# A streaming-encoder block with SwiGLU: where silu's product and the feature sums of the pair behind stand among the quarter products

## Chip, core and metric

One core of a Trainium2 chip runs the whole block in one launch. The metric is the device time of one execution in microseconds. The kernel before took 1066.19 us (median of 3 runs, 1064.51 to 1068.32).

## Reference

The block is one layer on 1024 tokens of width 1024, all in float32. The change lies in the second half, the SwiGLU:

```python
h2 = rmsnorm(x, norm2_g[layer])
gate = jnp.einsum('bsd,df->bsf', h2, w_gate[layer])
up = jnp.einsum('bsd,df->bsf', h2, w_up[layer])
x = x + jnp.einsum('bsf,fd->bsd', jax.nn.silu(gate) * up, w_down[layer])
```

`d` is 1024 and `f` is 2816. Ahead of it stand the norm, the input projection, the attention with forget gates, the pooling mixer and the output projection, and behind it a last norm.

## The kernel before

Every float32 operand of a matmul is split into a high part (a copy by ScalarE, L120) and a low part (the difference, by VectorE, L121); a product is three matmuls (L161 to L163: high by high, high by low, low by high). Such a pair of parts of one weight operand is called a page. There are three page buffers, so a page takes the place of the one three pages earlier, once TensorE has read that.

Gate and up are made with Strassen's method in Winograd's form: seven products of blocks, called P1 to P7, with sums of blocks as operands. The 2816 features go in eleven pairs of 128-wide groups, `j` from 0 to 10. For a pair the raw weights of gate and up arrive by DMA (`gu_raw`, issued by SyncE), GpSimd makes the four weight sums s1 to s4 of the pair ahead (`gu_sums`, L1091; s4 is the last), and the pages of the products follow one by one (`next_page`, two steps ahead in the list `todo`). Index n is 0 for gate and 1 for up.

The products accumulate in PSUM banks: c1 takes P1, P6 and P5, c3 takes P7 and P4. Between them ScalarE copies what is needed to SBUF (`snap`, L1154: sP1, sU2 and sU4 for n = 0 and 1). From banks and copies `corner` makes the features: VectorE adds bank and copy (L1178 for gate, L1180 for up), ScalarE applies silu (L1179) and GpSimd multiplies (`done`, L1181). This gives h22 and h21. h11 is multiplied at L1314. h12 is multiplied by VectorE (L1340) after silu (L1338), in `features`. GpSimd then makes the four feature sums f1 to f4 for the down projection (`feature_sum`, L1190: f1 needs h12 and h22, f2 needs f1 and h11, f3 needs h11 and h12, f4 needs h21 and f2). `spill` stores features in DRAM through ScalarE's DMA queue. Copies, features and sums share a ring of 11 buffers; the copies of sU2 have one buffer for each n, and silu of h21 is written over the copy of sU2 with n = 0.

The products P2 and P3 are done once more by the same method, as seven quarter products Q1 to Q7 with 256 columns (`fine_product`). Their results go through three banks called fineA (Q1, Q6, Q5, Q3 in turn), fineB (Q7, then Q4) and fineC (Q2). A bank keeps accumulating, so VectorE adds each stand of it to the copies in SBUF (L1288), and the next quarter product on that bank must wait for this addition. The operand quarters are summed in place by VectorE (`fine_sums`, L1245: one sum in part "a", ahead of the page P2a; three in part "b", ahead of the page P2b).

From pair 3 on (`BOTH = 3`) a pair runs the order LAST, with P2's quarters woven into P6, and P3's into P4:

```python
LAST = ("P1", "P7", "P2a", "P6", "P2b", "P5", "P3a", "P4", "P3b")
```

At step P2a TensorE does Q1, Q2, Q7, a quarter of P6, Q4, another quarter of P6 and Q6; at step P6 the second half of P6 and Q5.

Each engine runs its instructions in the order of its queue. A planner sets that order ahead of time; `tc.issue_after(ins)` demands that an instruction stands behind `ins` in the queue of the same engine. Before the change, the work around step P1 of a pair was issued so: `features(j - 1)` first, then page P2a with its sum "a"; page P6 at step P7; the three sums "b" at step P2a. GpSimd multiplies h22 (pairs 3 to 9) and h21 (pairs 2 to 10) behind s4.

Of the kernel before, what the change touches and what calls it, by code (L numbers as in the profile page):

```python
# [30 lines left out]
NG = NF // 2  # L31
# [14 lines left out]
def tile_kernel(  # L46
# [16 lines left out]
    nc = tc.nc  # L63
# [24 lines left out]
    def bank(name, tag, bufs, n=1):  # L88
# [11 lines left out]
        out=wmask[:, S - P :],  # L100
# [16 lines left out]
    mark = {}  # L117
# [683 lines left out]
    op = op_g.__enter__()  # L801
# [273 lines left out]
    BOTH = 3  # L1075
# [81 lines left out]
    feats = {}  # L1157
    ready = {}
    pending = []
# [7 lines left out]
    def corner(j, name, key, src, to):  # L1167

        h = feature(j, name, to)
        if key == "sU2" and j >= BOTH - 1:  # L1170
            q = snaps[j, key, 0]
        else:
            q = wk_tile("q" if key else "e2", 1, f"q{name}_{j}")
        if key is None:
            nc.scalar.activation(out=q, in_=banks[src, 0], func=AF.Silu)
            nc.vector.tensor_tensor(out=h, in0=banks[src, 1], in1=q, op=ALU.mult)
        else:
            nc.vector.tensor_tensor(out=q, in0=banks[src, 0], in1=snaps[j, key, 0], op=ALU.add)  # L1178
            nc.scalar.activation(out=q, in_=q, func=AF.Silu)  # L1179
            mark[name, j] = nc.vector.tensor_tensor(out=h, in0=banks[src, 1], in1=snaps[j, key, 1], op=ALU.add)  # L1180
            done = lambda: nc.gpsimd.tensor_tensor(out=h, in0=h, in1=q, op=ALU.mult)  # L1181
            if name == "h22" and BOTH <= j < NG - 1:
                pending.append(done)
            else:
                with tc.issue_after(mark["s4"].ins) if name == "h21" and j >= BOTH - 1 else ExitStack():
                    done()

    def feature_sum(j, name, key, a, b, op):
        t = feature(j, name, key)
        nc.gpsimd.tensor_tensor(out=t, in0=feats[a], in1=feats[b], op=op)  # L1190

    QTR = (slice(0, 256), slice(256, 512))
    fine = {}
# [137 lines left out]
    def features(j, *behind):  # L1331

        if j:
            acc = [snaps[j, "sU4", n] for n in range(2)]
            with ExitStack() as order:
                for ins in behind:
                    order.enter_context(tc.issue_after(ins.ins))
                nc.scalar.activation(out=acc[0], in_=acc[0], func=AF.Silu)  # L1338
            with tc.issue_after(mark["page"].ins):
                nc.vector.tensor_tensor(out=acc[1], in0=acc[1], in1=acc[0], op=ALU.mult)  # L1340
            feats["h12"] = acc[1]
        feature_sum(j, "f1", "P5", "h12", "h22", ALU.add)
        feature_sum(j, "f2", "P6", "f1", "h11", ALU.subtract)
        feature_sum(j, "f3", "P7", "h11", "h12", ALU.subtract)
        if j:
            feature_sum(j, "f4", "P3", "h21", "f2", ALU.subtract)

# [69 lines left out]
    def next_page(j, k):  # L1417
        if (j, k) not in pages:
            if k[-1] in "ab":
                pages[j, k] = fine_page(j, k[:2], k[-1])  # L1420
            else:
                pages[j, k] = gu_page(f"gu{j}_{k}", operands[j][k])
        if j + 1 < NG:
            if k in ("P3", "P3a"):
                gu_raw(j + 1, 0)
            if k == "P4":
                gu_raw(j + 1, 1)
            if k == ("P3b" if j else "P4"):
                operands[j + 1] = gu_sums(j + 1)
                while pending:  # L1430
                    with tc.issue_after(mark["s4"].ins):
                        pending.pop(0)()

    PACE = {(1, "P1"): 3, (1, "P2"): 3, (2, "P1"): 2, (2, "P2"): 2, (2, "P6"): 3, (2, "P7"): 3}
    waiting = []
    for i, (j, k) in enumerate(todo):
        shown = mark["page"]
        if j >= BOTH and k == "P2a":
            fine_sums(j, "P2", "b")
        elif i + 2 < len(todo) and (j < BOTH or k != "P1"):  # L1440
            with ExitStack() as order:
                if j >= BOTH and k == "P3b":
                    order.enter_context(tc.issue_after(mark["add"].ins))
                if j >= BOTH and k in ("P7", "P6", "P2b", "P5"):
                    if k == "P5":
                        fine_sums(j, "P3", "b")
                    for name in ("page", "hi") + (("sum",) if k in ("P2b", "P5") else ()):
                        order.enter_context(tc.issue_after(mark[name].ins))
                next_page(*todo[i + 2])
            if j >= BOTH and k == "P6":  # L1450
                with tc.issue_after(mark["page"].ins):
                    fine_sums(j, "P3", "a")
            if k == "P2b":
                mark["P3a"] = mark["page"], mark["hi"]
        waiting.append(spills[:])
        spills.clear()
        if j < BOTH:
            while len(waiting) > 1:
                with tc.issue_after(mark["hi"].ins), tc.issue_after(mark["snap"].ins) if j == 2 else ExitStack():
                    spill(waiting.pop(0))  # L1460
        elif k in ("P7", "P3a", "P4", "P3b"):
            rest = sum(waiting, [])
            due = [e for e in rest if e[1] < j and (k != "P7" or e[0] in ("P1", "P4"))][: 8 if k == "P3b" else 2]
            waiting[:] = [[e for e in rest if e not in due]]
            with tc.issue_after(mark["hi"].ins):
                spill(due)
        if i == 1:
            product(j, k, 0, (0, 1))
            with tc.issue_after(mark["turn", ORDER[-1]].ins):
                product(j, k, 0, (2, 3))  # L1470
                product(j, k, 1)
        elif k in window[j]:
            step, little, whole = window[j][k]
            acc = [snaps.get((j, dict(P2="sP1", P3="sU4")[little], n)) for n in range(2)]
            deep = j >= BOTH and (j, little) != (NG - 1, "P3") or (j, k) == (BOTH - 1, "P3b")
            for piece in NEXT[k] if deep and k in NEXT else (PIECES2 if deep else PIECES)[step]:
                with tc.issue_after(mark["mm"].ins):
                    if isinstance(piece, str):
                        fine_product(j, little, piece, acc)
                    elif isinstance(piece[0], str):  # L1480
                        product(j + (k == "P3b"), *piece)
                    else:
                        product(j, whole, *piece)
                if (k, piece) == ("P2a", "Q7"):
                    with tc.issue_after(mark["Q7"].ins):
                        next_page(j, "P2b")
        elif i:
            for n in range(2):
                with tc.issue_after(mark["mm"].ins) if j >= BOTH or j == BOTH - 1 and k != "P1" else ExitStack():
                    product(j, k, n)  # L1490
        if (j, k) == (NG - 1, "P3b"):
            last_features = lambda j=j, k=k: after(j, k)
        else:
            if j >= BOTH and k == "P1":
                features(j - 1)
                with tc.issue_after(mark["add"].ins), tc.issue_after(mark["h21", j - 1].ins):
                    next_page(*todo[i + 2])
            after(j, k)
        if j == NG - 1:
            if k == "P1":  # L1500
                for par in range(2):
                    down_raw(0, par)
            if k == "P6":
                for par in range(2):
                    down_load(par)
            if k == "P2b":
                for key in ("P5", "P6", "P7", "P4"):
                    down_sum(0, key)
            if k == "P3a":
                with tc.issue_after(mark["add"].ins), tc.issue_after(mark["hi"].ins):  # L1510
                    down_page(0)
        if (j, k) == (0, "P4"):
            t = const.tile([P, 2, 2, 256], R, tag="wmask", bufs=1, name="fine1_b22")
            q7 = small(wk, "e2", "fine3h_b22"), small(xw, "junk2", "fine3l_b22")
            finer += fine_steps("b22", (t[:, 0, :, :], t[:, 1, :, :]), q7, ("e0", "e1"))
        if (j, k) == (BOTH - 2, "P3b"):
            q5, q7 = ([small(wk, f"g{n + m}", f"fine{n}{m}_b21") for m in range(2)] for n in (2, 4))
            finer += fine_steps("b21", q5, q7, ("g0", "g1"))
        for _ in range(min(PACE.get((j, k), 2 if j < 2 else 0), len(finer))):
            with tc.issue_after((shown if j == 2 else mark["page"] if j else mark["h22", 0]).ins):  # L1520
                finer.pop(0)()
        pages.pop((j, k))
# [184 lines left out]
```

## Time and profile before

| | |
|---|---|
| median of the runs | 1066.19 us |
| the profiled execution's own time | 1069.82 us |
| its span, first to last instruction | 1068.0 us |
| TensorE busy | 1035.7 us (97%) |
| VectorE busy | 804.0 us (75%) |
| ScalarE busy | 470.6 us (44%) |
| GpSimd busy | 408.5 us (38%) |
| mean granted TensorE clock | 0.986 |

The page of the profile gives busy times over the whole span. PE is TensorE, PEld its weight loads, DVE VectorE, ACT ScalarE, POOL GpSimd, SP SyncE; a q behind a name is the engine's DMA queue. In rows of waits stand the waiting instruction, what it waited for, the total in us, the number of times and the longest. Rows of stretches give the start and end, the length, busy time and instructions of PE, PEld, DVE, ACT and POOL, then the granted clock, the share of DMA and GB/s. Rows of the timeline give start, duration, engine, line, operation, output and inputs, and in brackets the idle time ahead with what ended it. In names the buffer numbers are left out: `gu_P` is a bank or a page of a product, `r` raw weights, `s` a weight sum, `sn_sU` and `sn_sP` copies, `f` and `h` features, and `fineB_6P` is the bank fineB in pair 6.

### The profile page before, as it was taken

The page shows a single profiled execution, that of the slowest core. Times are in us where ns is not written, and L with a number is a line of the kernel's source. Part 1 is how long each engine was busy: PE and PEld are TensorE (multiplying, and loading weights), DVE is VectorE, ACT ScalarE, POOL GpSimd, SP SyncE. Part 2 cuts the span into 40 slices and gives each one's busy share as a digit, 9 for nine tenths or more (in the row PEclk, how much of TensorE's full clock was granted, in tenths as well). Part 3 has the DMA queues.
Part 4 walks back from the last instruction along what each step waited for, and adds up shares of the span by engine and source line. Part 5 has one row for each costly group of instructions (what it writes and reads, how often), then busy time and mean ns, then how long its engine had stood idle before and what let it go on. Part 6 is the DMA issues. An engine that isn't in the chain of part 4 may idle for free.

```text
span 1068.0 us, 15171 instructions
## 1 busy us (share of the span) xinstructions
PE 1035.7 (97%) x5428; PEld 886.4 (83%) x5428; DVE 804.0 (75%) x1222; ACT 470.6 (44%) x759; POOL 408.5 (38%) x319
## 2 busy tenths in 40 slices
PE   9999999999999999999998998988989999999997
PEld 8988888998888888887787887877877888888886
DVE  7465566676885598979767767778678999888887
ACT  7334365665674276344233232432342433333445
POOL 4450121213452150844734826637538530000035
PEclk9999999999999999999999989998999999999999
DMA  6224334234931251423141332332216684354424
GB/s 243 51 64 140 84 95 103 60 100 103 331 92 50 91 168 55 141 72 108 41 129 60 109 119 69 109 111 69 97 60 226 225 317 147 119 178 147 149 89 158
DMA packets 108795, 130.28 MB, mean 122 GB/s; under 512 B 8040, under 2 KB 71024, under 8 KB 108720
## 3 DMA queue, kind: packets, MB, share of 16 engines
q1 hardware_dynamic: 97216, 108.18, 32.3%
q10 hardware_dynamic: 10784, 19.16, 4.7%
q0 software_dynamic: 720, 1.97, 0.5%
q8 instruction: 43, 0.70, 0.3%
q14 instruction: 32, 0.26, 0.1%
HBM read 86.29 MB, written 33.03 MB: 112 GB/s over the span
## 4 chain that ended last, share of the span: by engine, by line
PE 77%; DVE 8%; POOL 5%; issue 4%; DMA 3%; ACT 1%; SPq 0%; POOLq 0%; ACTq 0%; DVEq 0%
PE d L161 6%; PE d L163 6%; PE d L162 6%; PE gu_P L161 6%; PE gu_P L162 6%; PE gu_P L163 6%; POOL s L1091 4%; PE po L657 3%; PE tp L643 3%; PE qk L162 3%; PE qk L161 3%; PE qk L163 3%; PE o L162 3%; PE o L163 3%; PE o L161 3%
## 5 line engine op out<-in xcount | busy, mean ns | idle before, releaser
L162 PE MATMUL d<-d,d 128*128 128x512 f32 (+1 forms) x308 | 119.2, 388 | 0.0
L163 PE MATMUL d<-d,d 128*128 128x512 f32 (+1 forms) x308 | 119.0, 388 | 0.0
L629 POOL TENSOR_SCALAR p<-p,rr 128x128 f32<-128x128 f32 (+3 forms) x64 | 48.8, 768 | 176.4 <-DVE rr L628 142.2
L161 PE MATMUL d<-d,d 128*128 128x512 f32 x308 | 108.0, 388 | 0.0
L120 ACT ACTIVATE d<-r_f 128x1536 fp32r<-128x1536 f32 (+1 forms) x28 | 38.7, 1383 | 111.4 <-PE d L162 111.4
L121 DVE TENSOR_TENSOR gu_P_l<-s,gu_P_h 128x1024 fp32r<-128x1024 f32 (+1 forms) x38 | 70.3, 1862 | 6.3 <-ACT gu_P_h L120 6.0
L162 PEld LDWEIGHTS d<-d,d 128*128 128x128 f32 x308 | 57.8, 188 | 12.1 <-DVE d L121 0.2
L163 PEld LDWEIGHTS d<-d,d 128*128 128x128 f32 x308 | 57.8, 188 | 11.9
L161 PEld LDWEIGHTS d<-d,d 128*128 128x128 f32 x308 | 57.8, 188 | 11.9
L1558 POOL TENSOR_SCALAR sse<-sse 128x1 f32<-128x1 f32 x7 | 3.5, 495 | 167.7 <-ACT junk L1554 167.7
L626 ACT ACTIVATE p<-p,mn 128x128 f32<-128x128 f32 (+3 forms) x64 | 49.4, 773 | 31.9 <-DVE mn L620 29.0
L1245 DVE TENSOR_TENSOR r<-r 128x256 f32<-128x256 f32 x32 | 45.4, 1437 | 15.8 <-POOL s L1091 15.5
L648 DVE TENSOR_TENSOR tl<-tp,th 128x512 fp32r<-128x512 f32 (+1 forms) x80 | 49.5, 633 | 9.5 <-ACT th L647 8.5
L1314 POOL TENSOR_TENSOR sn_sP<-sn_sP,sn_sP 128x512 f32<-128x512 f32 x8 | 10.5, 1306 | 108.9 <-ACT sn_sP L1313 108.9
L121 DVE TENSOR_TENSOR d<-r_f,d 128x1536 fp32r<-128x1536 f32 (+1 forms) x28 | 46.4, 1658 | 6.8 <-ACT d L120 6.7
L163 PE MATMUL qk<-hTh,l_qk 128*128 128x512 f32 x128 | 50.7, 396 | 0.0
L161 PE MATMUL qk<-hTh,h_qk 128*128 128x512 f32 x128 | 50.6, 395 | 0.0
L1662 DVE TENSOR_TENSOR x2f_s<-d,x2f_s 128x512 f32<-128x512 f32 x64 | 42.4, 684 | 10.8 <-PE d L163 10.8
L162 PE MATMUL qk<-hTl,h_qk 128*128 128x512 f32 x128 | 50.4, 394 | 0.0
L647 ACT ACTIVATE th<-tp 128x512 fp32r<-128x512 f32 (+1 forms) x80 | 42.4, 550 | 16.4 <-PE tp L643 13.5
L121 DVE TENSOR_TENSOR gu_P_l<-r,gu_P_h 128x1024 fp32r<-128x1024 f32 x24 | 42.7, 1783 | 7.8 <-ACT gu_P_h L120 4.6
L620 DVE CUSTOM_DVE_ANT_0 p<-z,wmask 128x128 f32<-128x128 f32 (+3 forms) x64 | 33.7, 535 | 13.6 <-PE z L618 9.7
(1179 smaller groups left out, 3427.3 us busy)
## 6 DMA issues: line engine op xcount, KB each, us to landing
r_f<-hsdP SPq DMA_DIRECT2D x77, 256.0 KB
r<-in_w_gate_dram SPq DMA_DIRECT2D x44, 256.0 KB
r<-in_w_up_dram SPq DMA_DIRECT2D x44, 256.0 KB
r_wd<-in_w_down_dram SPq DMA_DIRECT2D x22, 512.0 KB
hsdP<-f ACTq DMA_DIRECT2D x40, 256.0 KB
s<-hi SPq DMA_DIRECT2D x64, 128.0 KB
hsdP<-h ACTq DMA_DIRECT2D x23, 256.0 KB
x<-in_x_dram SPq DMA_DIRECT2D x8, 512.0 KB
```

What stands on the lines that cost most here:

```text
L120: mark["hi"] = nc.scalar.activation(out=hi, in_=src, func=AF.Copy)
L121: return eng.tensor_tensor(out=lo, in0=src, in1=f32(hi), op=ALU.subtract)
L161: nc.tensor.matmul(ps, lh, rh, start=start, stop=False, **kw)
L162: nc.tensor.matmul(ps, lh, rl, start=False, stop=False, **kw)
L163: mark["mm"] = nc.tensor.matmul(ps, ll, rh, start=False, stop=stop, **kw)
L626: nc.scalar.activation(out=pr[:, :n], in_=pr[:, :n], func=AF.Exp, scale=-1.0, bias=mn, accum_out=rs)
L629: nc.gpsimd.tensor_scalar(out=pr[:, :n], in0=pr[:, :n], scalar1=rr, scalar2=1.0, op0=ALU.mult, op1=ALU.mult)
L647: nc.scalar.activation(out=th[:, :w], in_=tp[:, :w], func=AF.Copy)
L648: nc.vector.tensor_tensor(out=tl[:, :w], in0=tp[:, :w], in1=f32(th[:, :w]), op=ALU.subtract)
L1091: at = nc.gpsimd.tensor_tensor(out=out, in0=in0, in1=in1, op=op)
L1245: mark["sum"] = nc.vector.tensor_tensor(out=out, in0=in0, in1=in1, op=op)
L1662: added = nc.vector.tensor_tensor(out=row, in0=ps, in1=row, op=ALU.add)
```

## The change

Four edits to the order, none to the arithmetic:

- `features(j - 1)` moves from the end of step P1 to step P7, behind page P6. VectorE's product for h12 and GpSimd's feature sums so stand behind P6's low part.
- The three later sums of P2's quarters move from step P2a to the end of step P1; page P6 stands behind them.
- On GpSimd, h22's product is issued at its corner, and the weight sums behind it (before: behind s4). h21's product of pairs 2 to 9 waits in `pending` until f3 of the next step P7, and f4 follows it (before: behind s4).
- In pair 2 the page for P7 stands behind the copies of sP1.

```diff
@@ corner @@
-            if name == "h22" and BOTH <= j < NG - 1:
+            if name == "h21" and BOTH - 1 <= j < NG - 1:
                 pending.append(done)
             else:
-                with tc.issue_after(mark["s4"].ins) if name == "h21" and j >= BOTH - 1 else ExitStack():
-                    done()
+                mark["done"] = done()
 
     def feature_sum(j, name, key, a, b, op):
         t = feature(j, name, key)
-        nc.gpsimd.tensor_tensor(out=t, in0=feats[a], in1=feats[b], op=op)
+        mark["f"] = nc.gpsimd.tensor_tensor(out=t, in0=feats[a], in1=feats[b], op=op)
@@ features @@
         feature_sum(j, "f3", "P7", "h11", "h12", ALU.subtract)
+        if pending:
+            with tc.issue_after(mark["f"].ins):
+                pending.pop(0)()
         if j:
             feature_sum(j, "f4", "P3", "h21", "f2", ALU.subtract)
@@ next_page @@
             if k == ("P3b" if j else "P4"):
-                operands[j + 1] = gu_sums(j + 1)
-                while pending:
-                    with tc.issue_after(mark["s4"].ins):
-                        pending.pop(0)()
+                with tc.issue_after(mark["done"].ins) if j >= BOTH else ExitStack():
+                    operands[j + 1] = gu_sums(j + 1)
@@ the loop over todo @@
-        if j >= BOTH and k == "P2a":
-            fine_sums(j, "P2", "b")
-        elif i + 2 < len(todo) and (j < BOTH or k != "P1"):
+        if i + 2 < len(todo) and (j < BOTH or k not in ("P1", "P2a")):
             with ExitStack() as order:
                 if j >= BOTH and k == "P3b":
                     order.enter_context(tc.issue_after(mark["add"].ins))
                 if j >= BOTH and k in ("P7", "P6", "P2b", "P5"):
                     if k == "P5":
                         fine_sums(j, "P3", "b")
-                    for name in ("page", "hi") + (("sum",) if k in ("P2b", "P5") else ()):
+                    for name in ("page", "hi") + (("sum",) if k in ("P2b", "P5", "P7") else ()):
                         order.enter_context(tc.issue_after(mark[name].ins))
+                if (j, k) == (BOTH - 1, "P2"):
+                    order.enter_context(tc.issue_after(mark["snap"].ins))
                 next_page(*todo[i + 2])
+            if j >= BOTH and k == "P7":
+                features(j - 1)
             if j >= BOTH and k == "P6":
                 with tc.issue_after(mark["page"].ins):
                     fine_sums(j, "P3", "a")
@@ the end of a step @@
             if j >= BOTH and k == "P1":
-                features(j - 1)
                 with tc.issue_after(mark["add"].ins), tc.issue_after(mark["h21", j - 1].ins):
                     next_page(*todo[i + 2])
+                fine_sums(j, "P2", "b")
             after(j, k)
```

## Prediction

> **What bounds the kernel now.** I read the head of the page first, then TensorE's own waits, since it is busy almost throughout, and then busy time and granted clock by stretches.
>
> ```profile
> span 1068.0 us, 15171 instructions
> ```
> ```profile
> PE fineB_5P L161 <- DVE sn_sP L1288: 2.8, 1, 2.8
> ...
> PE fineB_9P L161 <- DVE sn_sP L1288: 2.8, 1, 2.8
> PE gu_P L161 <- ACT sn_sP L1154: 1.8, 1, 1.8
> PE fineB_3P L161 <- DVE sn_sP L1288: 1.8, 1, 1.8
> ```
>
> TensorE waits for another engine at few places, and they are the same place: in each of the pairs 3 to 10 (the eight that run the order LAST) the quarter product Q4 of P2 waits for VectorE's addition of Q7. Bank B must be read before Q4 accumulates on it. Seven times the wait is 2.8 us (the first and the last row of the seven stand here), once it is 1.8; together 21.4 us. One other wait of 1.8 us is in pair 2. The next view shows that the idle time isn't all.
>
> ```profile
> 575.30:616.10 40.80, 37.99 (x204) 32.32 (x204) 31.14 (x37) 14.34 (x19) 22.54 (x11) 0.99 0.30 97
> ...
> sum 295.00, PE 275.21 PEld 234.75 DVE 217.54 ACT 100.35 POOL 159.26; mean PE 39.32 PEld 33.54 DVE 31.08 ACT 14.34 POOL 22.75
> ```
> ```profile
> 575.30:578.70 3.40, 3.40 (x21) 3.05 (x22) 2.59 (x4) 1.66 (x2) 0.00 (x0) 1.00 0.38 107
> ...
> 616.10:622.10 6.00, 5.97 (x20) 5.30 (x21) 3.25 (x5) 1.66 (x2) 0.00 (x0) 0.50 0.60 175
> ...
> 659.60:663.00 3.40, 3.40 (x12) 2.92 (x13) 2.12 (x3) 1.06 (x1) 0.00 (x0) 0.50 0.42 122
> ...
> 701.70:705.10 3.40, 3.36 (x20) 3.04 (x21) 2.58 (x4) 1.66 (x2) 0.00 (x0) 1.00 0.38 110
> ```
> ```profile
> 488.90:492.40 3.50, 3.50 (x10) 2.72 (x9) 3.50 (x3) 0.00 (x0) 3.42 (x2) 0.51 0.22 84
> ```
>
> The first fence cuts the time from the end of one such wait to the end of the next, for seven pairs (length, TensorE's busy time, and near the end the granted clock). A pair with clock 0.99 keeps TensorE busy for 37.99 us; the seven together last 295.0 and keep it busy for 275.2. So about 9 us of busy time are slow time. The other fences show it: behind four equal waits of 2.8 us the clock is 1.00, 0.50, 0.50 and 1.00, and it is 0.51 behind the wait in pair 2. Where it is halved, 3.4 us hold 12 matmuls in place of 20. Whether a wait costs clock seems to hang on where it falls, but half clock follows these waits. All else in these pairs is dense: the limit of the stage is 38.0 us a pair.
>
> Why is Q7's addition late? VectorE works in order.
>
> ```profile
> 689.65 1.50 DVE L1245 TENSOR_TENSOR r<-r 128x256 f32<-128x256 f32 x1 [1.96 <-POOL s L1091]
> 691.07 1.78 DVE L1340 TENSOR_TENSOR sn_sU<-sn_sU,sn_sU 128x512 f32<-128x512 f32 x1
> 692.78 1.21 DVE L121 TENSOR_TENSOR gu_P2a_l<-r,gu_P2a_h 128x1024 fp32r<-128x1024 f32 x1
> 694.02 1.40 DVE L1245 TENSOR_TENSOR r<-r 128x256 f32<-128x256 f32 x1
> 695.35 2.31 DVE L121 TENSOR_TENSOR gu_P_l<-s,gu_P_h 128x1024 fp32r<-128x1024 f32 x1
> 697.58 2.91 DVE L1245 TENSOR_TENSOR r<-r 128x256 f32<-128x256 f32 x2
> 700.41 0.41 DVE L1288 TENSOR_TENSOR sn_sP<-fineA_7P,sn_sP 128x256 f32<-128x256 f32 x1
> ...
> 701.27 0.41 DVE L1288 TENSOR_TENSOR sn_sP<-fineB_7P,sn_sP 128x256 f32<-128x256 f32 x1
> ```
> ```profile
> 678.05 2.41 POOL L1091 TENSOR_TENSOR s<-r,r 128x1024 f32<-128x1024 f32 x1 [3.60 <-DMA r<-in_w_up_dram]
> ...
> 690.83 1.48 POOL L1181 TENSOR_TENSOR h<-h,sn_sU 128x512 f32<-128x512 f32 x1
> 693.00 2.14 POOL L1190 TENSOR_TENSOR f<-sn_sU,h 128x512 f32<-128x512 f32 x1 [0.69 <-DVE sn_sU L1340]
> ...
> 698.77 1.44 POOL L1190 TENSOR_TENSOR f<-h,f 128x512 f32<-128x512 f32 x1
> ```
> ```profile
> 659.31 0.95 DVE L121 TENSOR_TENSOR gu_P2b_l<-r,gu_P2b_h 128x768 fp32r<-128x768 f32 x1
> ...
> 661.96 1.22 DVE L121 TENSOR_TENSOR gu_P_l<-s,gu_P_h 128x1024 fp32r<-128x1024 f32 x1 [0.51 <-ACT gu_P_h L120]
> 663.11 0.42 DVE L1245 TENSOR_TENSOR s<-s 128x256 f32<-128x256 f32 x1
> 664.12 0.42 DVE L1288 TENSOR_TENSOR sn_sP<-fineA_6P,sn_sP 128x256 f32<-128x256 f32 x1 [0.60 <-PE fineA_6P L163]
> ```
> ```profile
> 673.15 1.30 POOL L1314 TENSOR_TENSOR sn_sP<-sn_sP,sn_sP 128x512 f32<-128x512 f32 x1 [15.23 <-ACT sn_sP L1313]
> ```
>
> The first fence is VectorE ahead of pair 7's wait, the second GpSimd in the same time, the third VectorE when GpSimd has nothing to do. The same 128x256 sum takes 0.42 us alone and 1.40 to 1.50 beside GpSimd's work; a low part (128x1024) takes 1.22 alone and 2.31 beside it. GpSimd's 512-wide operation takes 1.30 alone and up to 2.14. The starts and ends fit one rule: a VectorE operation with all operands in SBUF and a GpSimd operation don't run together, and each waits for the other's current one. The additions from PSUM (0.41) don't suffer. So six operations that need about 5 us take 11, and Q7's addition comes 2.8 us late.
>
> **The change, part by part** (times of pair 7's rows).
>
> *The corner's products.* h22's product was behind the four weight sums; now it stands ahead of them, h21's stands behind f3. GpSimd is free until its data land at 678.05:
>
> ```profile
> 675.71 0.68 DVE L1180 TENSOR_TENSOR h<-gu_P,sn_sU 128x512 f32<-128x512 f32 x1
> ```
>
> h22's last input is there at 676.4, the product ends near 677.8: nothing, hidden by the wait for the weights; without that cover it would cost up to 1.3 us of a chain with 2.7 us to spare (next step). The sums still end near 689.6.
>
> *VectorE from 689.65.* GpSimd now has nothing until the h12 product (L1340) is done, and that stands behind P6's low part. So VectorE runs alone: first sum 0.42, to 690.1; ScalarE's high part (row below) to 691.25; low part of P2a 1.21, to 692.5; three later sums at 0.42, to 693.7; P6's low part 1.22, to 694.9; L1340 to 695.6 at 0.7 (half of a low part's columns, so half of 1.22 and a little overhead; at most the 1.78 above). Its silu is needed by 694.9 and ended at 688.4 (L1338 below). TensorE and ScalarE:
>
> ```profile
> 695.16 0.28 PE L161 MATMUL fineA_7P<-b21h,gu_P2a_h 128*128 128x256 f32 x1
> ...
> 697.31 0.40 PE L161 MATMUL gu_P<-t2h,gu_P_h 128*128 128x512 f32 x1
> ```
> ```profile
> 687.73 0.63 ACT L1338 ACTIVATE sn_sU<-sn_sU 128x512 f32<-128x512 f32 x1 [3.65 <-DVE sn_sU L1288]
> 691.27 1.06 ACT L120 ACTIVATE gu_P2a_h<-r 128x1024 fp32r<-128x1024 f32 x1 [2.90 <-DVE r L1245]
> ```
>
> Q1, Q2 and Q7 run from 695.16 to 697.31, 0.72 each. P2a's page has 2.7 us to spare in place of 1.2, and P6's low part 2.4. Q7's addition runs about 697.5 to 697.9. A quarter of P6 follows, 6 matmuls of 0.23, so 1.38, and Q4 is wanted at 698.7: the wait of 2.8 goes, with 0.8 to spare. Q4 (0.72), 1.38, Q6 (0.72), P6's second half (2.76), Q5 (0.72) and P5 follow: Q6 is wanted at 700.8, Q5 at 704.27, P5 at 705.0.
>
> *What is late next.* GpSimd's five operations (f1, f2, f3, h21, f4) now begin at 695.75 instead of 693.00, take 6.5 us alone and 8.7 at the slower rows' rate (from 693.00 to 700.21 for four, and 1.48), so they end between 702.3 and 704.5. Beside them now run P2b's low part, P5's low part and P3's first sum, which were alone before. Taking turns: f1 to 697.05, f2 to 698.35, P2b's low part to 699.2 (wanted by Q6 at 700.8), f3 to 700.4; P5's high part (1.06) follows Q4 (699.4) and ends near 700.6, h21 is ahead of its low part and ends at 701.7, the low part at 702.8 (wanted at 705.0), f4 at 704.05, P3's sum at 704.25, Q6's addition 704.6. In the third fence above Q6's addition stood behind that sum too. Q5 accumulates on bank A, is wanted at 704.27 and needs this addition: a new wait of 0.35 us. If P5's low part gets its turn before h21 it is 0; if each turn is 0.2 later, 0.9. I take 0.35, as the turns are those of the rows: 8 x 0.35 = 2.8 us back. It is far from the 1.8 us behind which the clock was seen to fall.
>
> *Others that wait.* h21's product reads the tile of silu that the next copy of sU2 overwrites. It ends at 701.7 (703.0 at the slow rate), the copy takes 0.6, and P5 wants its bank at 705.0: nothing, with 1.4 us to spare at worst. The store of h21 is the first that the moved work feeds:
>
> ```profile
> 673.64 0.39 ACTq L1292 DMA_DIRECT2D hsdP<-h  x1
> ```
>
> That is pair 6's row. h21's new end lies some 42 us ahead of pair 7's, at 659.4 to 660.7, and f1 to f4, in their old order, are stored behind it: 13 us of cover for a shift of 3 to 11 us. The loads in SyncE's queue wait for low parts that come no later than before.
>
> *Pair 2.* P7's page moves behind the copies of sP1.
>
> ```profile
> 485.49 1.99 ACT L120 ACTIVATE gu_P_h<-s 128x1024 fp32r<-128x1024 f32 x2
> 487.38 0.57 ACT L1154 ACTIVATE sn_sP<-gu_P 128x512 f32<-128x512 f32 x1
> ```
>
> The copy can begin at 485.5 and free the bank at 486.1, where TensorE ran dry at 486.2: the wait shrinks by 1.5 (at most 1.8, at least 0), and with it the half clock of 3.5 us, worth 1.7: together 3.2 us. P7's high part comes 1.1 us later, and isn't used for another product of 5 us.
>
> **Sum**, against the profiled execution's 1069.8 us (span 1068.0): seven pairs 295.0 - 7 x 37.99 = 29.1; pair 3's idle wait 1.8; pair 2 3.2; new wait -2.8. Together 31.3, so 1038.5. The median of the runs, 1066.2, is 3.6 below the profiled execution: **1035 us**. With the bounds (pair 2 nothing, 0.9 a pair: 1066.2 - 30.9 + 7.2 = 1042.5; no new wait, pair 2 in full: 1066.2 - 30.9 - 3.5 = 1031.8) and 2 us for the spread of runs, this case reaches from 1030 to 1044.
>
> **Rivals.**
>
> 1. *The clock doesn't follow these waits.* If the half clock came from something else, only idle time would return: 21.4 + 1.5 - 2.8 = 20.1, so 1046. Against it: half clock stands right behind waits and nowhere else in these pairs. For it: two equal waits had none. The Trainium skill, "TensorE: Matmul & The Clock Gate", Part 1, says that the clock falls after at least one idle window of about 3.4 us; by that rule gaps of 1.8 and 2.8 us should cost no clock, and the time would be this rival's. The traces go against it: 0.50 behind 2.8 us, 0.51 behind 1.8.
> 2. *The wait moves to Q5 or P5.* If GpSimd's chain runs a turn or two later than I have it, Q6's addition or the sU2 copy comes 1.8 us or more late, and the clock falls again: 8 x (1.8 + 1.7) = 28 lost, 1066.2 - 34.1 + 28 = 1060. With a wait of 1.8 alone 1046. For it: the spare times are 0 to 1.4 us.
> 3. *Slower: L1340 falls behind P2b's low part.* The change orders it behind P6's low part only; if the planner puts it behind the three additions and P2b's low part, it ends at 699.6 and f1 to h21 run to about 708 (four operations of 1.3 and three turns of 1.0). The copy of sU2 then ends at 708.6, and P5 waits 3.6 us, and loses 1.7 of clock behind it, in each pair: 8 x 5.3 = 42 lost against 34 won, 1074. It decides from an h21 that ends at 707.0, 4 us behind my slow end (then 2.6 of wait and 1.7 of clock, 8 times, are the 34 won). Against it: the product has all inputs at 694.9, a microsecond before the first addition.
> 4. *The order doesn't change*, because the planner had freedom left: 1066.
>
> **How the numbers follow.** A measurement of this kernel can tell about 0.3% (3 us) from no change. Forecast 0.77; rival 1 0.06; rival 2 0.09; rival 3 0.05; rival 4 0.03. Rivals 1 and 2 are still faster by over 0.3%: faster 0.92, same 0.03, slower 0.05. The range is the forecast's with rival 1 and the lower end of rival 2, and the spread of runs below: 1029 to 1047.
>
> **What would show it.** In the profile after: no waits of Q4 in TensorE's list, pairs of 38.0 to 38.4 us at clock 1.00, VectorE's sums at 0.42 and low parts at 1.22 ahead of Q1, GpSimd idle between the weight sums and f1. A wait of fineA for the PSUM addition confirms the step on what is late next; one of gu_P for the sU2 copy shows rival 2 or 3. Half clock without waits would be rival 1. I am wrong if Q4 still waits.

## The result and the profile after

The changed kernel takes 1040.41 us (median of 4 runs, 1038.89 to 1041.42) against 1065.35 before (median of 4 runs, one more than above; 1064.23 to 1068.32): a ratio of 0.976, 95% interval 0.9735 to 0.9786. The profiled execution took 1039.63 us, its span is 1037.9. The forecast was 1035, from 1029 to 1047.

TensorE's own waits in the kernel after, without those under 1 us:

```profile
PE fineB_10P L161 <- DVE sn_sP L1287: 2.0, 1, 2.0
PE gu_P L163 <- DVE gu_P_l L121: 1.3, 2, 0.9
PE warm L254 <- DVE junk L252: 1.2, 1, 1.2
PE fineA_10P L161 <- DVE sn_sP L1287: 1.1, 1, 1.1
```

The eight waits of Q4 are gone. There are two new ones in pair 10: P2's Q5 waits 1.1 us (bank A) and P3's Q7 2.0 us (bank B). Two more are for the low parts of late pages, 0.9 us for P7 in pair 2 and 0.4 us for P1 in pair 3 (the row with 1.3). Where the time went is read best from three stretches, cut at the start of Q1 in pair 3 and of Q1 in pair 10. Before:

```profile
0.00:527.55 527.55, 523.51 (x2911) 454.62 (x2912) 372.73 (x747) 270.34 (x515) 196.88 (x192) 1.00 0.37 111
527.55:821.50 293.95, 275.22 (x1429) 234.75 (x1428) 216.49 (x253) 100.35 (x133) 156.39 (x76) 0.96 0.30 99
821.50:1068.00 246.50, 237.00 (x1090) 197.01 (x1088) 214.78 (x224) 99.94 (x111) 55.26 (x52) 1.00 0.49 173
```

After:

```profile
0.00:525.10 525.10, 521.63 (x2912) 452.57 (x2912) 371.29 (x749) 270.37 (x515) 191.40 (x188) 1.00 0.37 111
525.10:789.52 264.42, 264.27 (x1429) 226.85 (x1428) 189.35 (x254) 100.40 (x133) 153.86 (x77) 1.00 0.34 110
789.52:1037.90 248.38, 238.58 (x1090) 198.40 (x1088) 213.43 (x221) 99.95 (x111) 57.73 (x54) 0.98 0.49 172
```

Seven pairs took 293.95 us and take 264.42, with TensorE busy for all but 0.15 of them and the clock at 1.00 (before: 0.96). VectorE does the same work there in 189 us instead of 216: 27 us of its busy time are gone; the experiments show that they were waiting for GpSimd. The last stretch is 1.9 us longer, although the wait of pair 10's Q4 (2.8 us) lay in it before: something new costs 4.7 us there. Of this, 1.6 us is half clock (0.50 from 811.3 to 814.7), which keeps TensorE busy for 238.58 us instead of 237.00.

VectorE ahead of pair 7's Q4 in the kernel after; GpSimd's four weight sums end at 670.3, as they ended at 689.6 before:

```profile
670.37 0.42 DVE L1244 TENSOR_TENSOR r<-r 128x256 f32<-128x256 f32 x1 [1.95 <-POOL s L1091]
672.00 1.23 DVE L121 TENSOR_TENSOR gu_P2a_l<-r,gu_P2a_h 128x1024 fp32r<-128x1024 f32 x1 [1.21 <-ACT gu_P2a_h L120]
673.26 1.22 DVE L1244 TENSOR_TENSOR r<-r 128x256 f32<-128x256 f32 x3
674.40 1.22 DVE L121 TENSOR_TENSOR gu_P_l<-s,gu_P_h 128x1024 fp32r<-128x1024 f32 x1
675.53 0.69 DVE L1339 TENSOR_TENSOR sn_sU<-sn_sU,sn_sU 128x512 f32<-128x512 f32 x1
...
678.29 0.42 DVE L1287 TENSOR_TENSOR sn_sP<-fineB_7P,sn_sP 128x256 f32<-128x256 f32 x1 [0.35 <-PE fineB_7P L163]
```

Each operation has its short duration, and Q7's addition now waits for TensorE (the bracket), not TensorE for it. It ends 8.4 us behind the weight sums, where the forecast had 8.3; before it was 12.1.

### The profile page after: what moved, and what is told of

Its sections match the earlier page's. It is cut to its first block, busy times and chain, and to the rows that moved or that the text cites. A ratio compares the mean times of both kernels' runs of the same rounds, so it can differ in the third digit from the quotient of the medians.

```text
span 1037.9 us, 15125 instructions
## 1 busy us (share of the span) xinstructions
PE 1024.5 (99%) x5428; PEld 877.8 (85%) x5428; DVE 774.1 (75%) x1222; ACT 470.7 (45%) x759; POOL 403.0 (39%) x319
## 4 chain that ended last, share of the span: by engine, by line
PE 88%; DVE 5%; issue 2%; POOL 2%; ACT 1%; DMA 1%; ACTq 0%; POOLq 0%; SPq 0%; DVEq 0%
PE gu_P L161 8%; PE gu_P L163 8%; PE gu_P L162 8%; PE d L161 6%; PE d L163 6%; PE d L162 6%; PE po L657 3%; PE tp L643 3%; PE o L161 3%; PE qk L161 3%; PE qk L162 3%; PE qk L163 3%; PE o L163 3%; PE o L162 3%; PE v L374 2%
## 5 line engine op out<-in xcount | busy, mean ns | idle before, releaser
L121 DVE TENSOR_TENSOR gu_P_l<-s,gu_P_h 128x1024 fp32r<-128x1024 f32 (+1 forms) x38 | 65.9, 1744 | 9.9 <-ACT gu_P_h L120 9.6
L162 PEld LDWEIGHTS d<-d,d 128*128 128x128 f32 x308 | 57.8, 188 | 12.1 <-DVE d L121 0.2
L120 ACT ACTIVATE gu_P_h<-s 128x1024 fp32r<-128x1024 f32 (+1 forms) x38 | 36.4, 964 | 32.4 <-PE fineB_3P L162 3.5
L643 PE MATMUL tp<-ident,p 128*128 128x128 f32 x288 | 43.2, 274 | 0.0
```

The source lines that it names most:

```text
L120: mark["hi"] = nc.scalar.activation(out=hi, in_=src, func=AF.Copy)
L121: return eng.tensor_tensor(out=lo, in0=src, in1=f32(hi), op=ALU.subtract)
L162: nc.tensor.matmul(ps, lh, rl, start=False, stop=False, **kw)
L643: nc.tensor.transpose(tp[:, w : w + P], probs[h, 2 * sb + a][:, s * P : (s + 1) * P], ident)
```

## Experiments

Theory A is that of the prediction: VectorE operations on SBUF and GpSimd operations hold each other up, and the order of VectorE's queue decides which of them fall into GpSimd's busy time.

**GpSimd's part alone.** On the kernel before, only h22's and h21's products move.

```diff
-            if name == "h22" and BOTH <= j < NG - 1:
+            if name == "h21" and BOTH - 1 <= j < NG - 1:
                 pending.append(done)
...
+        if pending:
+            with tc.issue_after(mark["f"].ins):
+                pending.pop(0)()
```

> The kernel before with one part of the change: on GpSimd h22's product stands ahead of the weight sums and h21's behind f3; the features, the later quarter sums and page P7 of pair 2 stay where they were. Theory A (VectorE and GpSimd take turns, and the order of VectorE's queue decides): without h22's product the first sum falls to 0.42 us and h12's product to 0.7, but f1 then begins 2 us earlier and takes its turns with P2a's low part, the later sums and P6's low part, with h21's product among them, so Q7's addition starts at about the same place (11.6 us behind s4, as before) and Q4 still waits 2 to 3.2 us in pairs 3 to 10: 1060 to 1072 us, the same as before. Rival (GpSimd's two products were what made VectorE late): the 2.1 us that these two operations save come off the wait, Q4 waits 0.7 us, too little for half clock: 1040 to 1048 us.

Measured: 1061.12 us (10 runs; before 1066.5), ratio 0.9954, 0.9935 to 0.9972. Q4 still waits 2.0 to 2.2 us in pairs 4 to 10, and 1.6 in pair 3. VectorE in pair 7:

```profile
683.35 0.43 DVE L1244 TENSOR_TENSOR r<-r 128x256 f32<-128x256 f32 x1 [1.96 <-POOL s L1091]
683.69 0.68 DVE L1339 TENSOR_TENSOR sn_sU<-sn_sU,sn_sU 128x512 f32<-128x512 f32 x1
684.98 1.85 DVE L121 TENSOR_TENSOR gu_P2a_l<-r,gu_P2a_h 128x1024 fp32r<-128x1024 f32 x1 [0.61 <-ACT gu_P2a_h L120]
686.76 2.31 DVE L121 TENSOR_TENSOR gu_P_l<-s,gu_P_h 128x1024 fp32r<-128x1024 f32 x1
688.99 4.36 DVE L1244 TENSOR_TENSOR r<-r 128x256 f32<-128x256 f32 x3
```

Of the 2.2 us that the first two operations save, 1.3 are lost again: 0.6 in a wait for ScalarE's high part, and 0.6 in P2a's low part, beside which f1 now runs. So 0.6 to 0.8 us come off Q4's wait, where theory A had about none and the rival all 2.1. Theory A's mechanism holds, and so does its range for the time, near the lower end: 0.5% is gained.

**VectorE's part alone.** The changed kernel with GpSimd's products behind s4 again, and without the edit in pair 2.

```diff
-            if name == "h21" and BOTH - 1 <= j < NG - 1:
+            if name == "h22" and BOTH <= j < NG - 1:
...
-                if (j, k) == (BOTH - 1, "P2"):
-                    order.enter_context(tc.issue_after(mark["snap"].ins))
```

> The changed kernel without its GpSimd part and without the edit in pair 2: features behind page P6 and the three later sums ahead of it, but h22's and h21's products behind s4. Theory A: h22's product costs the first sum 1.1 us of turns, h21's one more turn at most; all operations ahead of Q7's addition still end by 696.6 on the clock of pair 7's rows, before the addition is wanted (697.5). Q4's wait is gone, clock 1.00 in pairs 3 to 9, h12's product ends 1 us later than in the changed kernel: 1040 to 1045 us (about 2.4 above the changed kernel, by pair 2). Rival (both parts are needed): Q4 still waits 1 us or more in each pair, 1050 us or more.

Measured: 1040.12 us, ratio 0.9756 (0.9731 to 0.978): the whole gain. Its seven pairs take 264.16 us. With the two products back behind s4, GpSimd ends them before the page of P2a is ready; h12's product in pair 7 ends 7.0 us behind the weight sums instead of 5.9, and nothing waits for it. The longest wait left is one of 2.9 us, P3's Q7 in pair 10. It comes although h21's product stands behind s4 as before; see "Pair 10" below.

**Without the feature sums.** The kernel before with its own order; the sums f1 to f4 of pairs 2 to 9 are left out.

```diff
     def feature_sum(j, name, key, a, b, op):
+        if BOTH - 1 <= j < NG - 1:
+            feats[name] = feats[a]
+            spills.append((key, j, feats[a]))
+            return
...
```

> The kernel before, order untouched, with the four feature sums of pairs 2 to 9 left out (their first operand is stored in their place). Theory A (taking turns with GpSimd makes VectorE late, not the number or the order of its own operations): the later sums fall from 1.4 to 0.42 us, P6's low part from 2.31 to 1.22, Q7's addition comes 3 to 4 us earlier, Q4 waits nowhere in pairs 3 to 9, and the half clock behind it goes: 1035 to 1046 us. Rival (VectorE's queue is too long ahead of Q1, whoever runs beside it): Q4 waits 1.5 us or more, 1055 us or more.

Measured: 1033.91 us (one run), no wait of Q4 in any pair. Beside an idle GpSimd the old order is fast enough:

```profile
675.48 1.22 DVE L121 TENSOR_TENSOR gu_P_l<-s,gu_P_h 128x1024 fp32r<-128x1024 f32 x1
676.62 0.76 DVE L1249 TENSOR_TENSOR r<-r 128x256 f32<-128x256 f32 x2
```
```profile
525.58:788.68 263.10, 263.10 (x1429) 227.52 (x1428) 189.60 (x253) 100.60 (x134) 107.87 (x49) 1.00 0.34 111
```

P6's low part takes 1.22 instead of 2.31, the last two sums 0.76 instead of 2.91. That settles the cause: not VectorE's own work or its number of operations, but GpSimd's feature sums beside it. (The first two operations, beside which GpSimd multiplies h22 and h21 here too, still take 1.50 and 1.78.) It also gives the floor of seven pairs, 263.1 us or 37.59 each.

**Without the edit in pair 2.**

```diff
-                if (j, k) == (BOTH - 1, "P2"):
-                    order.enter_context(tc.issue_after(mark["snap"].ins))
```

> The changed kernel without the edit that puts page P7 of pair 2 behind the copies of sP1. Theory A: the wait of 1.8 us for the copy comes back in pair 2 with about 3.4 us of half clock behind it (1.6 us), while the new wait of 0.9 us for P7's low part goes; pair 3's Q1 starts 2 to 3 us later than in the changed kernel and the time is 2 to 3 us above it (1042 to 1044). Rival: the edit only trades one wait for another, pair 3's Q1 starts within 0.5 us of the changed kernel's.

Measured: 1041.08 us (one run). From the last matmul of pair 2's P2 to Q1 of pair 3, in the kernel before, after, and in this one:

```profile
485.78:527.55 41.77, 39.92 (x188) 33.30 (x187) 31.83 (x38) 16.55 (x24) 28.03 (x15) 0.96 0.24 80
```
```profile
484.78:525.10 40.32, 39.00 (x189) 32.10 (x187) 31.27 (x40) 16.40 (x24) 22.56 (x11) 1.00 0.23 79
```
```profile
487.38:527.66 40.28, 38.61 (x189) 32.09 (x188) 31.24 (x40) 16.25 (x24) 23.08 (x11) 1.00 0.25 83
```

The rival was right, measured from the end of P2. (Q1 itself starts 2.6 us later here, but the stages ahead are already late by as much.) The wait of 1.7 us for the copy returns, the waits for P7's and P1's low parts (0.9 and 0.4) go, and the stretch is as long; the time lies among those of the changed kernel. In this run the same wait left the clock at 1.00; before it was followed by half clock. So the edit gains nothing against this run, and 1.45 us against the kernel before.

**Pair 10.** What holds up VectorE there? These are VectorE and GpSimd of the kernel after:

```profile
801.24 2.83 DVE L121 TENSOR_TENSOR gu_P3a_l<-s,gu_P3a_h 128x1024 fp32r<-128x1024 f32 x1
804.10 5.38 DVE L1244 TENSOR_TENSOR s<-s 128x256 f32<-128x256 f32 x3
```
```profile
800.59 2.39 POOL L1377 TENSOR_TENSOR sumP<-r_wd,sumP 128x1024 f32<-128x1024 f32 x1
802.95 3.39 POOL L1377 TENSOR_TENSOR sumP<-r_wd,r_wd 128x1024 f32<-128x1024 f32 x1
806.29 2.58 POOL L1377 TENSOR_TENSOR sumP<-r_wd,sumP 128x1024 f32<-128x1024 f32 x1
```

Three sums that take 1.22 us in other pairs take 5.38. GpSimd makes the first sums of the down weights (`down_sum`) in pair 10 alone. Before the change these four began 1.6 us ahead of Q4, while TensorE waited, and ended 11.5 us behind its start. Now, behind the later feature sums, they run from 2.8 to 15.8 us behind it. The same three sums of VectorE before, and the first of GpSimd's four:

```profile
837.31 3.31 DVE L1245 TENSOR_TENSOR s<-s 128x256 f32<-128x256 f32 x3
```
```profile
826.47 2.55 POOL L1375 TENSOR_TENSOR sumP<-r_wd 128x1024 f32<-128x1024 f32 x1
```

They were held up then too, by 2.1 us, but no wait followed. Three kernels were run together on one chip: the changed kernel again; the sums moved behind h21's product, to step P4; and that with P3's first quarter sum behind Q6's addition.

```diff
-            if k == "P2b":
-                for key in ("P5", "P6", "P7", "P4"):
-                    down_sum(0, key)
+            if k == "P4":
+                with tc.issue_after(mark["done"].ins):
+                    for key in ("P5", "P6", "P7", "P4"):
+                        down_sum(0, key)
```

```diff
             if j >= BOTH and k == "P6":
-                with tc.issue_after(mark["page"].ins):
+                with tc.issue_after(mark["page"].ins), tc.issue_after(mark["add"].ins):
                     fine_sums(j, "P3", "a")
```

> The changed kernel once more, as the measure for the next two on the same chip: 0.976 of the time before, waits of 1.1 and 2.0 us in pair 10 and none of 1 us or more in pairs 3 to 9.

> The changed kernel with the first four sums of the down weights (pair 10, GpSimd) moved behind h21's product of pair 10, from step P2b to step P4. Theory A (pair 10's new waits come from these sums: they run while VectorE makes P5's and P3a's low parts and P3's quarter sums, and each of those waits for a sum of 2.4 to 3.4 us): P3's three later sums fall from 5.4 to 1.3 us, both waits in pair 10 go (1.1 to under 0.4, 2.0 to 0) and the half clock behind the second with them (1.6): 4 to 5 us less than the changed kernel, 0.971 to 0.973 of the time before. If the sums now hold up the low parts at the start of the down projection, part of it is lost there. Rival (pair 10 is late because h21's product and f4 come later, not by the sums): the waits stay, 0.976.

> The kernel with the later down sums, and P3's first quarter sum ordered behind Q6's addition on VectorE. Theory A (the small gap ahead of Q5 is Q6's addition standing behind that sum, which stands behind GpSimd): the gap of 0.03 to 0.25 us ahead of Q5 in pairs 3 to 9 goes to under 0.05, pairs of 37.6 in place of 37.6 to 37.95: about 1 us less, within what a time can tell; the trace decides. Rival (Q5 waits for something else): the gaps stay.

Measured: 1040.19 us (0.9753, 0.9739 to 0.9766); 1048.48 (0.9829, 0.9816 to 0.9843); 1047.59 (0.9821, 0.9807 to 0.9834). The cause was right: with the sums moved, pair 10's waits fall from 1.1 and 2.0 to 0.4 and 0, and the three sums take 1.22 us. But the place was wrong, and both kernels are 7 to 8 us slower than the changed one. The first kernel, the repeat, shows how much the half clock matters: it has the same two waits in pair 10, but its clock stays at 1.00, and the last stretch takes 246.90 us instead of 248.38:

```profile
791.80:1038.70 246.90, 237.06 (x1090) 197.29 (x1088) 213.63 (x221) 99.91 (x111) 57.75 (x54) 1.00 0.49 173
```

The waits of the second kernel from pair 10 on, and where they come from:

```profile
PE d L162 <- DVE d L121: 7.7, 1, 7.7
PE d L161 <- ACT d L120: 1.2, 1, 1.2
PE fineA_10P L161 <- DVE sn_sP L1287: 0.4, 1, 0.4
```
```profile
828.93 7.75 DVE L121 TENSOR_TENSOR d<-r_f,d 128x1024 fp32r<-128x1024 f32 x1
```
```profile
827.21 2.41 POOL L1377 TENSOR_TENSOR sumP<-r_wd,sumP 128x1024 f32<-128x1024 f32 x1
829.57 1.27 POOL L1189 TENSOR_TENSOR f<-sn_sU,h 128x512 f32<-128x512 f32 x1
830.79 2.37 POOL L1377 TENSOR_TENSOR sumP<-r_wd,sumP 128x1024 f32<-128x1024 f32 x1
833.13 1.25 POOL L1189 TENSOR_TENSOR f<-f,sn_sP 128x512 f32<-128x512 f32 x1
834.35 1.25 POOL L1189 TENSOR_TENSOR f<-sn_sP,sn_sU 128x512 f32<-128x512 f32 x1
```

One low part of 1.2 us took 7.75: it ended at 836.7, 1.1 us behind the fifth GpSimd operation in a row. The third kernel does what was expected of it: the gap ahead of Q5 is gone, and its seven pairs take 263.11 us, the floor (264.50 in the second kernel, which differs in that order alone).

**The sums on VectorE.** With P3's first sum behind Q6's addition, the four sums go to VectorE (`eng = nc.vector`), behind Q3's addition of pair 10; once on the changed kernel, once on VectorE's part alone.

```diff
-            if k == "P2b":
-                for key in ("P5", "P6", "P7", "P4"):
-                    down_sum(0, key)
+            if k == "P3b":
+                with tc.issue_after(mark["add"].ins):
+                    for key in ("P5", "P6", "P7", "P4"):
+                        down_sum(0, key)
```

> The changed kernel with Q6's addition ahead of P3's first quarter sum, and the first four down sums made by VectorE behind Q3's addition of pair 10 instead of by GpSimd. Theory A (a GpSimd operation beside VectorE's own SBUF operations holds them up, wherever it is put, so work on VectorE in a free stretch is cheaper): no wait of 0.3 us or more in pairs 3 to 10, pairs of 37.6, no wait of 7 us at the start of the down projection; the changed kernel's pair 10 waits (3.1), its Q5 gaps (about 1.2) and part of the half clock come off: 3 to 6 us below it, 0.969 to 0.973 of the time before. Rival (VectorE has no room there for four more sums of 1.2 us): TensorE waits for low parts at the start of the down projection for 3 us or more, 0.975 or above.

> The same two edits on the kernel that has VectorE's part of the change alone (GpSimd's products behind s4 as before, pair 2 as before). Theory A (GpSimd's part and pair 2's edit are worth nothing): the same time as the other kernel of this call within 0.2%. Rival (the moved GpSimd products leave room that matters once the other waits are gone): 3 us or more above it.

Measured: 1040.60 us (0.975, 0.9734 to 0.9766) and 1040.44 (0.9751, 0.9735 to 0.9768). The rival of the first was right on the place: pair 10 is clean, but the down projection waits 3.1 us for an addition that stands behind these sums, and 1.0 for a low part. For the second theory A holds: GpSimd's part and pair 2's edit add nothing here either.

Last, two of the sums (P5, P6) go behind the addition of P3's Q7, where VectorE was idle for 2.3 us, and P7's and P4's each behind the low parts of the page ahead of theirs.

```diff
-            if k == "P2b":
-                for key in ("P5", "P6", "P7", "P4"):
-                    down_sum(0, key)
             if k == "P3a":
+                with tc.issue_after(mark["Q7"].ins):
+                    for key in ("P5", "P6"):
+                        down_sum(0, key)
...
+        if (b, k) in ((0, "P2"), (0, "P6")):
+            with tc.issue_after(lows[0].ins), tc.issue_after(lows[1].ins):
+                down_sum(0, dict(P2="P7", P6="P4")[k])
```

> Like the kernel with the four down sums on VectorE behind Q3's addition, but two of them (P5, P6) stand in pair 10 behind the addition of P3's Q7, where VectorE was idle for 2.3 us, and P7's and P4's sums each stand behind the low parts of the page ahead, in the down projection. Theory A (VectorE has room for them, only not between P1's additions and P6's page): the waits of 3.1 and 1.0 us at the start of the down projection go to under 0.5 in all, with the half clock behind them (1.6), and pair 10 stays free of waits: 4 to 6 us below the changed kernel, 0.969 to 0.972 of the time before. Rival (the start of the down projection is bound by VectorE and GpSimd's feature sums in any order): TensorE waits there for 2 us or more, 0.974 or above.

Measured: 1035.27 us (1034.82 to 1037.85), ratio 0.9721 (0.9699 to 0.9742). Theory A held: the two waits left from pair 3's Q1 on are 0.5 us in pair 10 and 0.2 in the down projection. The stretches:

```profile
526.67:789.75 263.08, 263.08 (x1429) 227.34 (x1428) 188.71 (x254) 100.40 (x133) 154.05 (x77) 1.00 0.34 110
789.75:1034.40 244.65, 237.21 (x1090) 197.13 (x1088) 211.45 (x225) 100.29 (x111) 46.88 (x50) 0.99 0.49 175
```

This version is faster than both kernels: 263.08 us against 264.42 for the seven pairs, and 244.65 behind them against 248.38, or 246.90 in the repeat without half clock. Its slowest run (1037.85) is faster than the fastest of the changed kernel (1038.89).

## Why the prediction was right, point by point

- *What bounds the kernel; turns with GpSimd; Q4's wait goes.* Right, in mechanism and place, shown by the two kernels with one part each and by the one without feature sums. Q7's addition came within 0.1 us of where it was put.
- *The floor of 38.0 us a pair.* 0.4 too high: the floor is 37.59. The row taken (37.99 at clock 0.99) still held slow time. That is 2.8 us more gain.
- *What is late next.* Q6's addition is, as forecast, behind P3's sum and GpSimd. A gap of 0.35 us a pair was forecast; seven pairs lost 264.42 - 263.11 = 1.3 us to it, 0.2 each. The later steps of that chain cost nothing: P5 has no wait.
- *Pair 2, 3.2 us.* Wrong. The step said that P7's late page costs nothing and that the half clock goes with the wait. The late pages cost 0.9 and 0.4 us of waits against 1.7 for the copy, and the half clock need not follow the copy's wait: the clock was 0.51 behind it in the kernel before and 1.00 in the run without the edit. Of the 3.2 us, 1.45 came against the kernel before and none against that run.
- *GpSimd's moved products at no cost.* Right, but the step "VectorE from 689.65" counted on GpSimd being free there, and that isn't needed: VectorE's order alone has the whole gain.
- *Pair 10* was not seen: the four down sums stand on GpSimd behind the feature sums, and a step that moves those moves these. 1.1 + 2.0 us of waits and 1.6 of half clock, 4.7 us in the profiled execution (the repeat had the waits without the half clock). It is rival 2's case in one pair, by a cause that it didn't name.
- *The sum.* Forecast for the profiled execution 1038.5, measured 1039.63. From pair 3 on: 295.0 - 7 x 37.59 = 31.9, pair 3's wait 1.8, less 1.3 for Q5 and 4.7 for pair 10, 27.7; the stretches show 27.65. Ahead of it, 1.45 in pair 2 and 1.0 in stages that the change doesn't touch. That forecast and result differ by only 1.1 us is in part luck: the floor, Q5 and the stages ahead gave 2.8, 1.5 and 1.0 us more than forecast, pair 2 and pair 10 1.75 and 4.7 less.
- *The median.* Most of the 5.4 us between forecast and result is the step that put the median 3.6 us below the profiled execution again: after the change it lies 0.8 above. The step took over a difference that goes with the half clock of one execution. The mean granted clock was 0.986 in the profiled execution of before; of 39 further executions of that kernel, beside the experiments, those with 0.994 took 1063.6 to 1064.7 us and those with 0.986 took 1069.5 and 1070.2. With little half clock left (0.996 to 0.999 after) there is no such difference to take over.
- *Rival 1, the clock and the Trainium skill's rule* ("TensorE: Matmul & The Clock Gate", Part 1). The half clock went with the waits: the seven pairs keep TensorE busy for 264.27 us instead of 275.22. The rival is refuted, and with it the rule as a bound on gaps: see below.
- *Rivals 3 and 4.* Neither came: h12's product stands right behind P6's low part (the row at 675.53), and the order changed.

## What to carry to other kernels

When one VectorE operation has two durations in a trace, look at what GpSimd does in the longer one, and move the operations that nothing waits for behind those that TensorE waits for, rather than making any of them faster. Then follow everything that stands in the moved engine's queue to the end of the loop, the last iteration above all: here it held work of the next stage. A wait of TensorE is to be priced with the slow clock that may follow it.

## What the hardware showed

**The clock looks at fixed stretches.** The half-clock times of the kernel before begin at 488.94, 533.31, 615.23, 659.60, 741.52 and 785.90, and their distances, 44.37 and 81.92 us in turn, are 13 and 24 times 3.413. Cut on that grid, the stretch with most of a wait, and the next one, for pairs 4, 5, 6 and 7 (after the length, TensorE's busy time; then the clock):

```profile
570.86:574.27 3.41, 1.60 (x8) 0.89 (x6) 3.41 (x4) 0.10 (x1) 2.91 (x2) 1.00 0.00 0
574.27:577.68 3.41, 2.38 (x14) 2.12 (x15) 2.50 (x6) 1.80 (x2) 0.00 (x0) 1.00 0.07 19
611.82:615.23 3.41, 1.47 (x6) 0.67 (x4) 3.39 (x4) 0.24 (x1) 2.78 (x2) 1.00 0.00 0
615.23:618.64 3.41, 2.51 (x9) 2.32 (x10) 2.05 (x4) 1.59 (x2) 0.00 (x0) 0.50 0.08 23
656.19:659.60 3.41, 0.60 (x3) 0.18 (x3) 3.31 (x6) 0.84 (x1) 1.73 (x2) 1.00 0.00 0
659.60:663.02 3.42, 3.42 (x12) 2.94 (x13) 2.14 (x3) 1.06 (x1) 0.00 (x0) 0.50 0.42 123
697.15:700.56 3.41, 1.75 (x9) 1.03 (x7) 3.41 (x4) 0.00 (x0) 3.06 (x2) 1.00 0.00 0
700.56:703.98 3.42, 2.24 (x13) 1.99 (x14) 2.50 (x6) 1.90 (x2) 0.00 (x0) 1.00 0.04 11
```

Waits of one length gave half clock or none by how they fell on the grid: 1.47 us of work or less in a stretch, and the next is at half clock; 1.75, and it is not; 1.60 was on the edge, for three other stretches with as much work were each followed by one at half clock (0.50):

```profile
485.52:488.94 3.42, 1.57 (x7) 0.97 (x6) 3.42 (x4) 2.93 (x5) 2.05 (x2) 1.00 0.61 194
529.90:533.31 3.41, 1.65 (x8) 0.96 (x7) 3.31 (x7) 0.84 (x1) 1.26 (x1) 1.00 0.00 0
738.11:741.52 3.41, 1.61 (x7) 0.80 (x6) 3.41 (x4) 0.10 (x1) 2.92 (x2) 1.00 0.00 0
```

The run with GpSimd's part alone bears this out on a grid of its own (half clock from 489.88): 1.25 to 1.62 us of work in a stretch were followed by half clock five times, 1.69, 1.75 and 1.81 were not. The place of the grid differs from execution to execution, and so does the half clock of one and the same kernel.

So a wait of 1.8 us can cost 1.7 more (a stretch of 3.41 us at half clock), and one of 2.8 need not. The row at 615.23 shows the dear case: the rest of the wait fell into the slow stretch, which holds only 2.51 us of work, and the next one was slow as well (the row of 6.00 us at 0.50 in the prediction). The Trainium skill ("TensorE: Matmul & The Clock Gate", Part 1) names one idle window of about 3.4 us; the length agrees with the grid, but about half of one idle was enough here.

**GpSimd doesn't always give a turn.** In pair 7 of the kernel before, a low part got in behind one GpSimd operation (2.31 us instead of 1.22). Behind five in a row another waited 6.5 us (the 7.75 us row; why it got no turn isn't shown). A forecast by strict turns can so come out too short.
